# A two-layer diffusion backbone on one core: second-layer attention with pairs of float32r parts, a first modulation in chunks, and a second layer planned late

## The chip, the cores and the metric

The kernel runs on one core of a Trainium2 chip. What counts is the device time of one execution in microseconds: 1668.15 us for the kernel before, the median of 3 runs (1667.54 to 1668.26). In what follows PE is TensorE's matmul stream, PEld its weight loads, DVE VectorE, ACT ScalarE, POOL GpSimd, and SP the engine that issues the DMAs.

## What is computed

Two layers (DEPTH = 2) work on 512 latent tokens and 256 context tokens of width 1024. Cut to what matters here:

```python
for li in range(DEPTH):
    m_lat = jnp.split(s_lat @ w_ada[li] + b_ada[li], 6, axis=-1)      # modulation, from silu(c)
    m_ctx = jnp.split(s_ctx @ w_ada[li] + b_ada[li], 6, axis=-1)
    h  = rms_norm(x, g_mix[li]) * (1.0 + m_lat[1]) + m_lat[0]
    hc = rms_norm(ctx, g_mix[li]) * (1.0 + m_ctx[1]) + m_ctx[0]
    p, pc = h @ w_in[li], hc @ w_in[li]                               # 1024 -> 9 x 256
    y = jnp.concatenate([fourier_mix(p[..., :G]),
                         diff_attention_latent(...),                  # 4 heads, softmax twice, minus lam
                         na_attention_latent(...),                    # 4 heads, neighbourhood + context
                         chunk_gmlp(...)], axis=-1)
    x = x + m_lat[2] * (y @ w_out[li])
    ...                                                               # the context too, in layer 0 only
    h = rms_norm(x, g_ffn[li]) * (1.0 + m_lat[4]) + m_lat[3]
    x = x + m_lat[5] * conv_ffn(h, ...)                               # 1024 -> 2 x 2816 -> 1024
```

Every attention head ends in a product of softmax weights W (queries by keys) with values V (keys by 64).

## The kernel before

**Numbers in two parts.** TensorE takes weights and activations as float32r. To keep float32 accuracy, each operand is split into a rounded part (`hi`, a copy to float32r on ScalarE) and the rest (`lo`, one subtraction on VectorE or GpSimd), and `mm3` makes three matmuls of each product: hi hi, hi lo, lo hi. Weights come as 128x512 tiles through SP's queue into `raw` (4 places), are split by `w_split` into `wq` (6 places) and are used in the order of one list, `wlist`. Each tile costs one ScalarE copy and one subtraction `wq<-raw,wq`, on GpSimd or VectorE. Only the product of softmax weights and values stands apart: `turn` transposes a 128x768 tile of W in blocks of 128x128 and copies it to float32, and `pv` multiplies it by V with plain float32 matmuls, 64 columns each. The profile counts each of those as two matmuls.

**Who sets the order.** Nothing is ordered at run time. While the program is built, a planner (`Sched`) plays all threads (generators such as `Attention.item`, `qk_post`, `unit`) against a table of costs, and writes out the instruction of the thread that could start first, priorities `PR` deciding between those within `slack`. An `Alt` lets it choose the engine: `copy` between ScalarE and VectorE, `sub` between VectorE and GpSimd, `bias_w` being the handicap of VectorE for the weights' subtractions. Each engine then runs its own fixed queue, in order, and waits by semaphores. So an instruction that is late holds up all that stands behind it on its engine.

**The main thread.** The strings `o0` and `o1` name the projections of a layer in PE's order. DK, DQ, DV are keys, queries and values of the differential attention, NK, NQ, NV those of the neighbourhood attention, GU and GV the gated MLP, FA and FC the two halves of Fourier mixing, OO the output projection. A letter behind gives the streams: `l` latent, `c` context, `i` latent then context, `j` context then latent. `unit` runs one of them: for each of 4 latent and 2 context tiles of 128 tokens, 8 chunks of the depth of 128, and 3 matmuls of 256 columns for each chunk. `DKj4` does so in four rounds of two chunks, so that it can begin when two chunks of `h` are there. Attention items run as threads of their own between the matmuls of the main thread. An item is 128 queries of a head: scores, maximum, exponential, transposition, product with V.

**Modulation.** Section s of the modulation is a 1024 x 1024 product with one vector for each stream. At the start `ada_first` brings section 1 (the scale) as rows for TensorE (`ada_rows`: 16 float32 matmuls `plain,svec` of 512 columns with 2 rows out) and section 0 (the shift) as transposed tiles for VectorE (`ada_wide`: a custom multiply-and-sum, `CUSTOM_DVE_ANT_0`, 32 of them), half of the 1024 outputs after the other. All later sections go the VectorE way, one 256 KB tile at each `pace` (every 5.5 us in layer 0, from 64.2 us on, and every 4.1 us for layer 1), two such instructions for a tile when both streams need it.

**Feed-forward.** `up` makes pairs of 128 channels, 3 x 8 matmuls of 512 and as many of 258 columns for each; `conv` and `gated` follow on ScalarE, VectorE and GpSimd. `down` sums groups of four such channels into x. The last `down` of layer 0 and the norm of layer 1 (`Norm`: squares, their sum by matmuls with ones, GpSimd's power, a broadcast by matmuls, then eight chunks) stand between the layers.

## Time and profile before

| what | value |
|---|---|
| median of 3 runs | 1668.15 us |
| the profiled execution: its time | 1666.4 us |
| its span, first to last instruction | 1664.6 us |
| PE busy | 1599.3 us (96%) |
| PEld busy | 1419.3 us (85%) |
| DVE busy | 1103.6 us (66%) |
| ACT busy | 749.1 us (45%) |
| POOL busy | 715.3 us (43%) |
| mean granted clock of TensorE | 0.983 |

The span is 1.8 us short of the execution's own time, and that execution is 1.75 us below the median of the runs. All instructions bear the line of one helper (L314, L329 in the changed kernel), so groups are told apart by operation and tile: `wq,rounded` or `rounded,wq` is a product of weights and activations, `rounded` alone scores, `plain` alone the product of softmax weights and values, `ident` and `identr` transpositions. A row with a busy time gives the sum over the group, then the mean duration of one, which overlaps that of its neighbours.

### The profile page before, as it was taken

The numbers are of one execution on the slowest core, as the hardware profiler recorded it, in microseconds if no ns is written. First come the engines' busy times: TensorE is split into PE (matmuls) and PEld (weight loads), VectorE is DVE, ScalarE is ACT, GpSimd is POOL, SyncE is SP. The second block draws the span as 40 slices with busy tenths as digits, with TensorE's granted clock in tenths as the row PEclk, the third lists the DMA queues.
The fourth block names the chain that finished last, engine by engine and source line by source line (L and its number), as shares of the span: only waits on it lengthen the run. The fifth ranks groups of instructions, "written<-read, shape, count | busy, mean of one in ns | idle before, by whom it ended". The sixth has DMA issues, their size and how long they took to land.

```text
span 1664.6 us, 27016 instructions
## 1 busy us (share of the span) xinstructions
PE 1599.3 (96%) x9932; PEld 1419.3 (85%) x9932; DVE 1103.6 (66%) x2170; ACT 749.1 (45%) x1478; POOL 715.3 (43%) x550
## 2 busy tenths in 40 slices
PE   6799999999898999999999999999999999999999
PEld 2699889998687888888888888899999888888887
DVE  7998997888899856555543359578666744334334
ACT  4447765763523223223132236475665644334331
POOL 4762635345344433323333247214246654444442
PEclk8899999999999999999999998999999999999999
DMA  8331322545344343343421131101325433223222
GB/s 275 122 108 46 102 77 84 169 149 176 109 147 151 124 135 121 128 132 127 122 82 64 63 116 41 51 27 52 115 83 167 158 103 99 95 95 101 95 96 88
DMA packets 101652, 183.03 MB, mean 110 GB/s; under 512 B 12176, under 2 KB 14864, under 8 KB 101520
## 3 DMA queue, kind: packets, MB, share of 16 engines
q1 hardware_dynamic: 101520, 181.31, 33.3%
q8 instruction: 78, 1.28, 0.3%
q14 instruction: 54, 0.44, 0.1%
HBM read 177.07 MB, written 4.19 MB: 109 GB/s over the span
## 4 chain that ended last, share of the span: by engine, by line
PE 75%; DVE 16%; DMA 3%; ACT 2%; issue 2%; POOL 1%; SPq 0%; ACTq 0%; POOLq 0%; DVEq 0%
PE banks L314 75%; DVE plain L314 10%; DVE wa L314 3%; DVE rounded L314 2%; ACT plain L314 1%; POOL wq L314 1%; DMA raw<-in_w_out_dram 1%; DMA wa<-in_w_adat_dram 1%; DVE wq L314 1%; SPq L314 0%; DMA plain<-in_w_adat_dram 0%; ACT wq L314 0%; DMA raw<-in_ffn_up_dram 0%; ACT rounded L314 0%; POOL plain L314 0%
## 5 line engine op out<-in xcount | busy, mean ns | idle before, releaser
L314 PE MATMUL banks<-rounded,wq 128*128 128x512 f32 (+2 forms) x5856 | 1099.4, 348 | 14.5 <-DVE plain L314 9.4
L314 PEld LDWEIGHTS banks<-rounded,wq 128*128 128x128 f32 x5856 | 938.0, 189 | 158.6 <-issue 13.3
L314 POOL TENSOR_TENSOR wq<-raw,wq 128x512 fp32r<-128x512 f32 x390 | 528.2, 1358 | 709.5 <-ACT wq L314 675.3
L314 ACT ACTIVATE wq<-raw 128x512 fp32r<-128x512 f32 x425 | 264.0, 626 | 359.0 <-PE banks L314 260.4
L314 PE MATMUL banks<-wq,rounded 128*128 128x256 f32 (+1 forms) x1980 | 276.1, 295 | 11.0 <-DVE rounded L314 6.0
L314 DVE SCALAR_TENSOR_TENSOR plain<-banks,conv,plain 128x769 f32<-128x769 f32 (+1 forms) x176 | 155.4, 883 | 187.9 <-ACT plain L314 185.4
L314 PEld LDWEIGHTS banks<-wq,rounded 128*128 128x128 f32 x1980 | 254.1, 197 | 18.8 <-DVE rounded L314 6.8
L314 DVE SCALAR_TENSOR_TENSOR plain<-banks,m,plain 128x512 f32<-128x512 f32 (+1 forms) x176 | 112.4, 639 | 160.0 <-PE banks L314 159.7
L314 DVE CUSTOM_DVE_ANT_0 wa<-wa,plain 128x512 f32<-128x512 f32 x160 | 140.3, 878 | 45.3 <-DMA wa<-in_w_adat_dram 43.6
L314 POOL TENSOR_TENSOR plain<-plain,mhalf 128x4 f32<-128x4 f32 (+2 forms) x74 | 95.7, 1298 | 119.2 <-DVE plain L314 92.0
L314 ACT ACTIVATE plain<-banks,conv 128x770 f32<-128x770 f32 (+1 forms) x88 | 77.9, 885 | 138.7 <-PE banks L314 132.5
L314 ACT ACTIVATE plain<-plain 128x256 f32<-128x256 f32 (+3 forms) x152 | 78.7, 536 | 131.9 <-DVE plain L314 122.4
L314 ACT ACTIVATE plain<-banks,plain 128x768 f32<-128x768 f32 (+4 forms) x189 | 112.9, 606 | 54.9 <-PE banks L314 39.7
L314 ACT ACTIVATE plain<-banks 128x256 f32<-128x256 f32 (+2 forms) x217 | 93.3, 445 | 83.7 <-PE banks L314 72.9
L314 DVE TENSOR_TENSOR plain<-plain 128x256 f32<-128x256 f32 (+4 forms) x166 | 110.8, 670 | 19.7 <-ACT plain L314 13.0
L314 ACT ACTIVATE rounded<-plain 128x512 fp32r<-128x512 f32 (+2 forms) x110 | 65.7, 603 | 82.5 <-DVE plain L314 58.1
L314 DVE TENSOR_TENSOR rounded<-plain,rounded 128x256 fp32r<-128x256 f32 (+2 forms) x108 | 88.2, 823 | 17.3 <-ACT rounded L314 16.4
L314 DVE TENSOR_REDUCE plain<-banks 128x1 f32<-128x768 f32 (+4 forms) x112 | 92.0, 835 | 10.6 <-PE banks L314 9.7
L314 DVE CUSTOM_DVE_ANT_0 plain<-wa,plain 128x512 f32<-128x512 f32 x96 | 86.5, 902 | 15.8 <-DMA wa<-in_w_adat_dram 15.7
L314 PE MATMUL banks<-plain 128*128 128x64 f32 x736 | 90.5, 270 | 0.1
L314 PEld LDWEIGHTS banks<-plain 128*128 128x128 f32 x736 | 88.9, 192 | 1.8 <-issue 0.5
L314 POOL TENSOR_TENSOR plain<-plain 128x256 f32<-128x256 f32 (+2 forms) x52 | 61.7, 1196 | 61.8 <-DVE plain L314 27.8
(69 smaller groups left out, 960.9 us busy)
## 6 DMA issues: line engine op xcount, KB each, us to landing
raw<-in_ffn_up_dram SPq DMA_DIRECT2D x184, 256.0 KB, 2.6
wa<-in_w_adat_dram SPq DMA_DIRECT2D x160, 256.0 KB, 2.8
raw<-in_ffn_down_dram SPq DMA_DIRECT2D x88, 256.0 KB, 2.5
raw<-in_w_in_dram SPq DMA_DIRECT2D x80, 256.0 KB, 2.6
raw<-in_w_out_dram SPq DMA_DIRECT2D x64, 256.0 KB, 2.8
plain<-in_na_bias_dram SPq DMA_DIRECT2D x16, 320.0 KB, 3.6
plain<-in_xT_dram SPq DMA_DIRECT2D x16, 256.0 KB, 4.4
plain<-in_w_ada_dram SPq DMA_DIRECT2D x16, 256.0 KB, 4.0
```

Of the source, the lines that this page charges most:

```text
L314: fn(*args, **kw)
```

## The change

**Second-layer attention.** With `pvr[1] = 1`, layer 1 (not layer 0) splits both factors of the product with V. `turn` writes the transposed weights as float32r (`PT`) and adds a subtraction on VectorE for the rest (`PL`), both in one of two fixed places (`pts`). `values` splits V of each head once, hi and lo side by side. `pv` makes two float32r matmuls of each key block, PT by 128 columns (hi and lo of V) and PL by 64, and a `scalar_tensor_tensor` on VectorE adds the two halves. 168 pairs of float32 matmuls become 336 float32r matmuls.

**Side by side.** A new token DP runs keys and values of the differential attention as one projection (`pair_unit`): matmuls of 512 columns for 256 keys and 256 values, in four rounds, in both layers.

**First modulation in chunks.** `start_loader` brings the first two sections in quarters of the outputs, each followed by the weights of one round of DP. The first two quarters go whole to TensorE (512 columns, both sections), the last two by halves (256 columns of section 1 to TensorE, section 0 to VectorE). The latents' x is loaded ahead of the context.

**Second layer planned late.** `later` swaps priorities and rules for all that comes after the last three `up` of layer 0, among them `bias_w` (1.9 before that point, 0.1 behind it; it was 1.0). 35 weight subtractions stood on VectorE and 390 on GpSimd; now 232 and 197 do, 123 of VectorE's in the last feed-forward. The last `down` of layer 0 is listed twice, once for each stream (4 more weight tiles). The pace of the modulation is 5.9 us from 17.8 us on in layer 0, and 4.9 us for layer 1. The planner's cost table has new numbers, and it plans around the case that VectorE and GpSimd both read the memory at once (`port`).

```diff
+     'o0': 'DPi DQi NKl NVl NVc GUj NKc FAj GVj NQj XX FCc FCl OOc OOl', 'lead': 5, 'ffn_s': [1, 0],
+               'ada': 5.31}, 'o1': 'DPj NVj DQl NKi2 GVl NQl GUl2 FAl XX FCl OOa OOb',
...
+    def start_loader(nq):
...
+        for q in range(4):
+            w = 512 if q < NOW["rows"] else 256
+            tiles = []
+            spawn(ada_rows(q, w, tiles), 0.3)
...
+            if w < 512:
+                tiles = []
+                spawn(ada_wide(0, 0, q // 2, 2, tiles, 2, q % 2 * 4, 4), 0.3)
...
+            for i in range(q * nq, (q + 1) * nq):
+                yield from w_load(i, True)
...
+        for ph in range(4):
+            for i, (s, h, t) in enumerate(jobs):
...
+                for k in (2 * ph, 2 * ph + 1):
+                    q = yield from W.get(k)
+                    hk = yield from h.get(k, part)
+                    pairs.append(((hk[0][:, c], hk[1][:, c]), q))
...
+                yield mm3(p, pairs, ph == 0, ph == 3)
...
+                if parts_:
+                    yield sub(PL[:, cs], p[:, 0:n], PT[:, cs], False)
...
+                    two_ = [T.matmul(p[:, 0:128], PT[:, c], self.vp[hd][:, k * 128:k * 128 + 128], start=(j == 0),
+                                     stop=(j == n - 1)),
+                            T.matmul(p[:, 0:64], PL[:, c], self.vp[hd][:, k * 128:k * 128 + 64], start=False, stop=False)]
...
+            if PL is not None:
+                yield V.scalar_tensor_tensor(dst, p[:, 64:128], r, dst, ALU.mult, ALU.add)
```

**Where instructions move, first place.** PE's queue at the start, before: `plain,svec` are the rows of section 1, `ident` the broadcast of the norm (128x128) and the turning of the section's result (128x2), `wq,rounded` the keys, then the values.

```order
L314 MATMUL banks<-plain,svec 2x512 x3
L314 MATMUL banks<-wq,rounded 128x256 x6
L314 MATMUL banks<-plain,svec 2x512 x2
L314 MATMUL banks<-ident,plain 128x128 x4
L314 MATMUL banks<-plain,svec 2x512
L314 MATMUL banks<-wq,rounded 128x256 x6
L314 MATMUL banks<-plain,svec 2x512
L314 MATMUL banks<-ident,plain 128x2 x4
L314 MATMUL banks<-wq,rounded 128x256 x438
```

The same place after the change; `plain,svec` of 2x512 are the first two quarters, of 2x256 the last two, and 128x512 is the new projection DP, of which 102 more matmuls follow the last row.

```order
L329 MATMUL banks<-ones,plain 128x1 x6
L329 MATMUL banks<-plain,svec 2x512 x10
L329 MATMUL banks<-ident,plain 128x2 x4
L329 MATMUL banks<-plain,svec 2x512 x6
L329 MATMUL banks<-ident,plain 128x128 x6
L329 MATMUL banks<-ident,plain 128x2 x4
L329 MATMUL banks<-plain,svec 2x256 x8
L329 MATMUL banks<-ident,plain 128x2 x2
L329 MATMUL banks<-wq,rounded 128x512 x36
L329 MATMUL banks<-plain,svec 2x256 x8
L329 MATMUL banks<-wq,rounded 128x512 x6
L329 MATMUL banks<-ident,plain 128x2 x2
```

A whole round of DP (36 matmuls of 512 columns) now stands ahead of the last quarter of the modulation; before, only 12 matmuls of 256 columns stood ahead of the last row of section 1, and 438 behind it.

**Second place.** PE's queue in the neighbourhood attention of layer 1, before: `rounded` of 256 and 384 columns are scores, `plain` of 64 columns the products with V, and `rounded,wq` of 512 columns matmuls of the Fourier projection FA, put between the items.

```order
L314 MATMUL banks<-rounded,wq 128x512 x6
L314 MATMUL banks<-ident,plain 128x128 x4
L314 MATMUL banks<-rounded 128x384 x2
L314 MATMUL banks<-rounded 128x256 x2
L314 MATMUL banks<-ident,plain 128x128 x4
L314 MATMUL banks<-plain 128x64 x4
L314 MATMUL banks<-identr,rounded 128x128 x8
L314 MATMUL banks<-ident,plain 128x128
L314 MATMUL banks<-identr,rounded 128x128 x6
L314 MATMUL banks<-rounded,wq 128x512 x6
L314 MATMUL banks<-plain 128x64 x5
L314 MATMUL banks<-rounded 128x256 x4
```

After, the same attention from its first scores on:

```order
L329 MATMUL banks<-wq,rounded 128x512 x24
L329 MATMUL banks<-rounded 128x256 x4
L329 MATMUL banks<-rounded 128x384 x2
L329 MATMUL banks<-rounded 128x256 x2
L329 MATMUL banks<-rounded,wq 128x256 x3
L329 MATMUL banks<-identr,rounded 128x128 x8
L329 MATMUL banks<-rounded,wq 128x256 x9
L329 MATMUL banks<-identr,rounded 128x128 x6
L329 MATMUL banks<-rounded 128x384 x2
L329 MATMUL banks<-rounded 128x256 x2
L329 MATMUL banks<-ident,plain 128x128 x4
L329 MATMUL banks<-rounded 128x256 x4
```

The last half of Fourier mixing (the first row) now stands ahead of all 16 items, and from here to their end PE's queue holds 15 matmuls with weights (12 of them in these rows) beside the items' own; the output projection, the next of the main thread, needs the items' results.

**Third place.** VectorE's queue in that same stretch, after the change; `rounded<-banks,rounded` are the new subtractions, `SCALAR_TENSOR_TENSOR` the new sum of the two halves, the first row adds the position bias to the scores, and `TENSOR_REDUCE` is the maximum of a row of scores.

```order
L329 TENSOR_TENSOR banks<-banks,plain 128x384
L329 RECIPROCAL plain<-plain 128x1
L329 TENSOR_TENSOR rounded<-banks,rounded 128x128
L329 SCALAR_TENSOR_TENSOR plain<-banks,plain 128x64
L329 TENSOR_REDUCE plain<-banks 128x1
L329 TENSOR_TENSOR rounded<-banks,rounded 128x512
L329 SCALAR_TENSOR_TENSOR plain<-banks,plain 128x64
L329 CAST rounded<-banks 128x512
```

Before, VectorE had of these only the bias, the maximum, the reciprocal and a part of the copies; the subtractions and sums stand in one queue with them now, so that each waits for its turn there.

## Rows read from the trace of the kernel before

**Rows 1.** The page's busy times of three engines: us, share of span, instructions.

```profile
PE   1599.3 (96%) x9932; PEld 1419.3 (85%) x9932; DVE 1103.6 (66%) x2170; ACT 749.1 (45%) x1478; POOL 715.3 (43%) x550
```

**Rows 2.** Stretches: length, PE, PEld, DVE, ACT, POOL busy us (count), clock, DMA share, GB/s.

```profile
20.00:40.00 20.00, 14.54 (x42) 3.67 (x43) 18.57 (x42) 6.57 (x14) 13.66 (x13) 0.83 0.90 296
40.00:60.00 20.00, 11.34 (x41) 5.70 (x41) 19.57 (x34) 6.54 (x11) 18.55 (x13) 0.74 0.57 186
...
100.00:380.00 280.00, 273.71 (x2207) 261.69 (x2206) 245.49 (x625) 187.16 (x469) 128.45 (x107) 1.00 0.34 109
...
440.00:560.00 120.00, 111.42 (x626) 95.82 (x627) 117.06 (x206) 39.00 (x54) 54.42 (x32) 1.00 0.44 139
...
980.00:1060.00 80.00, 70.45 (x480) 66.50 (x479) 62.41 (x143) 41.02 (x82) 46.25 (x33) 0.89 0.23 79
1060.00:1320.00 260.00, 254.26 (x2035) 245.28 (x2034) 186.32 (x381) 168.37 (x374) 107.00 (x87) 0.99 0.28 93
1320.00:1664.60 344.60, 340.02 (x1509) 281.45 (x1507) 145.46 (x179) 131.47 (x211) 158.24 (x122) 1.00 0.29 99
```

**Rows 3.** PE in order of time, the start: start, length, matmuls, [idle before <-releaser].

```profile
27.65 1.02 PE L314 MATMUL banks<-plain,svec 128*2 128x512 f32 x2
...
35.57 1.87 PE L314 MATMUL banks<-plain,svec 128*2 128x512 f32 x2 [0.71 <-DMA plain<-in_w_ada_dram]
...
58.73 16.51 PE L314 MATMUL banks<-wq,rounded 128*128 128x256 f32 x119 [0.74 <-DVE rounded L314]
```

**Rows 4.** PE in order of time: two unbroken streams, and the neighbourhood attention's ends.

```profile
74.83 38.08 PE L314 MATMUL banks<-wq,rounded 128*128 128x256 f32 x316
...
376.68 41.16 PE L314 MATMUL banks<-rounded,wq 128*128 128x512 f32 x186
...
1182.16 0.84 PE L314 MATMUL banks<-rounded 128*128 128x384 f32 x4
...
1235.51 1.00 PE L314 MATMUL banks<-plain 128*128 128x64 f32 x8
```

**Rows 5.** DVE in order of time: two equal instructions of the first modulation.

```profile
16.80 0.69 DVE L314 CUSTOM_DVE_ANT_0 plain<-plain 128x512 f32<-128x512 f32 x1
...
48.45 1.76 DVE L314 CUSTOM_DVE_ANT_0 plain<-plain 128x512 f32<-128x512 f32 x1
```

**Rows 6.** What PE waited for, 440 to 560 us: sum, times, longest.

```profile
PE banks L314 <- DVE plain L314: 8.1, 5, 1.7
```

**Rows 7.** The page's costliest groups: the later modulation on VectorE.

```profile
L314 DVE CUSTOM_DVE_ANT_0 wa<-wa,plain 128x512 f32<-128x512 f32 x160 | 140.3, 878 | 45.3 <-DMA wa<-in_w_adat_dram 43.6
```

**Rows 8.** What PE waited for, 980 to 1060 us.

```profile
PE banks L314 <- DVE plain L314: 4.1, 2, 3.4
PE banks L314 <- DVE wq L314: 3.0, 2, 2.3
```

**Rows 9.** PE groups by form, 990 to 1320 us: count, busy, mean ns, idle before.

```profile
L314 PE MATMUL banks<-plain 128*128 128x64 f32 x336 | 40.7, 270 | 0.0
L314 PE MATMUL banks<-ident,plain 128*128 128x128 f32 x220 | 36.0, 283 | 1.2 <-POOL plain L314 1.1
...
L314 PE MATMUL banks<-rounded 128*128 128x256 f32 x48 | 8.7, 291 | 0.0
...
L314 PE MATMUL banks<-identr,rounded 128*128 128x128 f32 x56 | 5.6, 248 | 0.0
L314 PE MATMUL banks<-rounded 128*128 128x384 f32 x16 | 4.5, 363 | 0.0
```

**Rows 10.** DVE groups by form, 990 to 1320 us.

```profile
L314 DVE TENSOR_TENSOR plain<-plain 128x256 f32<-128x256 f32 x44 | 26.8, 614 | 9.3 <-ACT plain L314 6.0 <-POOL plain L314 3.0
L314 DVE TENSOR_TENSOR wq<-raw,wq 128x512 fp32r<-128x512 f32 x21 | 20.6, 979 | 16.7 <-ACT wq L314 16.5
...
L314 DVE TENSOR_TENSOR rounded<-banks,rounded 128x512 fp32r<-128x512 f32 x8 | 5.4, 687 | 4.7 <-ACT rounded L314 4.7
...
L314 DVE TENSOR_SCALAR plain<-banks,plain 128x64 f32<-128x64 f32 x5 | 1.4, 284 | 4.0 <-PE banks L314 4.0
```

More of the change, by code (lines that the diff above doesn't have):

```diff
@@ L619, in ada_fin, with ada_wide @@
             done.add((li, sec, c))
[L621 removed]
+    def ada_wide(li, sec, hf, ns, tiles, step=4, i0=0, n=8):
         acc_ = yield sm()
@@ L627, in ada_wide @@
             prod = yield k2()
-        for i in range(8):
-            yield lambda: len(tiles) > i and sbc[0] is not None
-            t = tiles[i]
+        for i in range(i0, i0 + n):
+            yield lambda: len(tiles) > i - i0 and sbc[0] is not None
+            t = tiles[i - i0]
             for st in range(ns):
@@ L737, in one @@
                 yield lambda: self.x[k] is not None
-                for j in range(self.parts):
-                    yield from self.add(k, j)
+                yield from self.add(k, 0, False)
             for k in range(8):
-                spawn(one(k), 0.5)
+                spawn(one(k), 0.1)
         def finish(self):
@@ L1177, in gate, with pt_slots @@
         left[0] -= 1
-    heads, items = Tokens(P["heads"]), Tokens(P["items"])
+    pts, at_work = [], {}
+    def pt_slots(li):
+        if NOW["pvr"][li]:
+            at_work[li] = 4 if li == 0 else 2
+            for i in range(NOW["slots"]):
+                pts.append((yield Req(sr, 1536, F32R)))
+    heads, items = Tokens(NOW["heads"]), Tokens(NOW["items"])
     class Attention:
@@ L1704, in start1, with later @@
         attn_all(1)
-    act(start1)
-    for tok in P["o1"].split():
-        token(1, tok)
-    ffn(1)
-    act(lambda: n1[1][0].drop_h())
+    def later():
+        NOW.update(P["later"])
+        PR.update(NOW["pr"])
+        n0[1] = [Norm(1, 0, s, drop=True, parts=1 if s else NOW["parts"][1]) for s in (0, 1)]
+        n1[1] = [Norm(1, 1, 0, parts=NOW["parts"][2])]
+        ffn(0, NOW["tail"] or [("down", 4), ("down", 5)])
+        act(start1)
+        tokens(1)
+        ffn(1)
+        act(lambda: n1[1][0].drop_h())
+        closed.append(True)
+    act(ada1)
+    ffn(0)
     def main():
```

372 lines of the change are left out of this document (247 added, 125 removed).

## The prediction

> **What bounds the kernel now.** The page's busy times come first: PE is at work for 1599 of 1665 us, and no other engine for more than 1104 [rows 1]. So the time is PE's work, plus the time in which PE stands still, plus what a lower clock costs, and each has to be found in its place. The table by stretches [rows 2] shows three such places. From 20 to 60 us PE is busy for 26 of 40 us, at a granted clock of 0.74 to 0.83, while the DMAs move 296 and then 186 GB/s: the start. From 440 to 560 us PE misses 8.6 us, and VectorE is busy for 117 of 120: the head of the first feed-forward, beside the modulation for layer 1. From 980 to 1060 us PE misses 9.6 us at a clock of 0.89: the change of layers. In the rest, 100 to 380 and 1060 to 1320 us, where all the attention is, PE misses 2% only, because weight products stand between the attention items; the last stretch is PE alone. A gain must come from the three places or from cheaper matmuls; a loss can come wherever PE stops being covered. The sum below is made against the profiled execution, 1666.4 us (span 1664.6 and 1.8 around it); the median of the runs is 1.75 above it.
>
> **1. The start, in chunks: -12 us.** Before, PE's unbroken stream starts at 58.7 us with 17 of the 288 matmuls of keys and values done [rows 3]. The next 119 last to 75.2, and the other 152 go at 38.08 / 316 = 120.5 ns [rows 4]: 18.3 us more, so keys and values are through at 93.2. After, the queue reads: 16 float32 rows of 512 columns, the norm's broadcast, 8 rows of 256 columns, a round of DP. VectorE is done with the sums of squares at 16.8 in both orders, since that takes all of x and ctx (its next instruction starts there [rows 5]). From 17 on the 16 rows take 1.02 us each when they follow each other, as the row at 27.65 does [rows 3]: 34. Broadcast and turning: 37. The 8 half rows: 41. The first chunks of h have by then gone through GpSimd, ScalarE and VectorE, which I put at 45. Then 144 matmuls at 41.16 / 186 = 221 ns [rows 4] are 31.9 us, and the last 8 half rows within them 4.1: 81. That is 12 us sooner, and the cheaper form of the projection is in it (288 x 120.5 against 144 x 221 ns: 2.9 us). The data allow it: by 45 us the queue must have brought x, ctx, three quarters of the modulation and two rounds of weights, some 11 MB; 296 GB/s [rows 2] bring 12 in 42 us. Ends: if the rows run at the 1.87 us of the row at 35.57 [rows 3], 13.6 us more, a loss of 2; if h is ready at 41, a gain of 16.
>
> **2. VectorE behind the start: +3 us.** Between 100 and 380 us VectorE is busy for 245 of 280 us [rows 2]. The change leaves its work in layer 0 about as it was (16 instructions of the first modulation less, 11 of the later sections more, a dozen others). The same 245 us in 12 us less are 92%. PE misses 2% at VectorE's 88% there and 7% at its 98% from 440 to 560 us [rows 2]; 92% lies at some 3%, and 1% more of 280 us is 3. Ends are 0 and all 12.
>
> **3. Head of the feed-forward: -6 us.** There PE waits 8.1 us for VectorE [rows 6]. Layer 1's modulation takes two instructions of 0.88 us [rows 7] for each tile there; a tile each 4.9 instead of 4.1 us takes 0.36 instead of 0.43 of VectorE, 8 us in the 120. The wait should nearly go. Next late is PE itself, so no more than 8.6 can be had; 0 is the other end.
>
> **4. Change of layers: -6 us.** 9.6 us idle and a clock of 0.89 on 70 busy us are some 17 us of loss [rows 2]. PE waits there for VectorE's norm (4.1 us) and for weight tiles that VectorE splits (3.0) [rows 8]. The norm's chain stays. But DP needs two chunks of h and two weight tiles for each round of 36 x 221 ns = 8 us, where the keys alone needed four chunks in each half. And the last `down`, listed twice, no longer holds four of the six places of split weights. Its four more tiles are hidden, at a DMA share of 0.23. I take a third of the loss; ends 0 and -12.
>
> **5. DP in layer 1: -3 us.** 288 x 120.5 - 144 x 221 ns = 2.9 us of PE, as in step 1.
>
> **6. The product with V: -6 us.** 336 float32 matmuls take 40.7 us [rows 9], 242 ns for a pair. No row has a float32r matmul of 128 or 64 columns on freshly loaded values. Nearest is the transposition `identr`, 128 float32r columns against a fresh 128x128 operand: 5.6 / 56 = 100 ns. Two of them make 200 ns, and 168 x 42 ns = 7 us; as 64 columns can hardly be dearer and accumulation may be, I take 6. Ends: each as dear as a 256-column matmul, 120.5 ns, gives 0; 192 columns at the 221 / 512 ns of the long stream give 83 ns for the two and a gain of 27. The Trainium skill ("TensorE: Matmul & The Clock Gate", section "Back-to-back issue gap") gives 81 ns as the sustained spacing of matmuls of 128 columns; by that this step would be worth 13 us, an estimate that the 100 ns of the row speak against.
>
> **7. Layer 1's attention: +13 us.** Here the change turns against itself. *VectorE's load.* From 1060 to 1320 us it is busy for 186 of 260 us [rows 2]. Added: some 50 of the 64 weight subtractions that come from GpSimd before layer 1's feed-forward, at up to 0.98 us, 50; 56 new subtractions from PSUM, at 0.69 us for 512 columns and less for the shorter ones, 31; 32 sums of halves, for which a 64-column operation at 0.28 is the nearest row, 9. Taken away: 21 additions of 256 columns at 0.61, which go to GpSimd, 13 [rows 10]. That makes 263 of 260. The price of 0.98 has GpSimd's weights beside it, though; at the 0.69 us of a subtraction of 512 columns from PSUM [rows 10], 84 weight subtractions are 24 us cheaper: 239. Such a load, 92 to 101%, is what the trace has from 440 to 560 us, where PE misses 7%. Over the first attention half, 130 us, that is 9 us against some 3 now. *The cover.* The neighbourhood items, from 1182 to 1236 us [rows 4], have weight products between them now; after, 15 such matmuls are left for 16 items. PE's own work on the items is 13.2 us of scores, 42 transpositions at 0.10, 80 at 36.0 / 220 = 0.164, 144 products at 0.10 [rows 9] and 1.8 for the 15: 47 us. The items took 54 us with VectorE less loaded, and nothing is queued behind but the output projection, which needs all of them. I put the stretch at 54 to 57, so PE stands still for 7 to 10 us where it did not before. Together 13 to 16, of which I take the lower; ends 0 and 30.
>
> **8. At no price.** In layer 1's feed-forward 121 weight subtractions move to VectorE: 118 us at 0.98 onto 145 busy of 345 [rows 2], a load of 76% beside a PE that is never short of weights there. If that cover failed, each late tile would cost what the split took, under 1 us.
>
> Sum: -12 + 3 - 6 - 6 - 3 - 6 + 13 = -17. 1666.4 - 17 = 1649.4, and 1.75 for the median: 1651. Its own range, from the middle halves of the ends, is 1643 to 1660.
>
> **Rivals.** *The attention stays covered.* VectorE's multiply-and-sum takes 0.69 us alone and 1.76 us at 48 us, when GpSimd is busy for 18.6 of 20 [rows 2, 5]. With most weights off GpSimd, VectorE's other work in layer 1 may shrink as much as the new work adds, and step 7 is 0: 1638. The Trainium skill ("SBUF — State Buffer", section "Who interferes with whom") says that a VectorE instruction with two inputs in SBUF waits for a GpSimd one that reads SBUF, for its whole length; by that rule just this happens, and the two rows agree with it. Against it stand the missing matmuls between the items, which no faster VectorE brings back. 17 in 100.
>
> *VectorE is layer 0's clock.* It is at 88% from 100 to 380 us and at 98% behind it. If it, not PE, sets when layer 0's attention and the first channels end, steps 1 to 3 bring nothing: 1668 - 6 - 3 - 6 + 13 = 1666. For it speaks that its work hardly shrinks; against it that PE misses only 6 us of 280 there. 12 in 100.
>
> *The chunks bring no earlier stream*, since rows at the slow price and DMA waits fill the time to 58 us: without step 1, and nothing to give back, 1660 to 1663. 8 in 100.
>
> *Slower: the clock falls in the uncovered items.* At the start, with PE waiting for DMAs and chunks, the granted clock was 0.74 [rows 2], near to halfway between TensorE's levels of 1.2 and 2.4 GHz. If the 16 items of layer 1 run at the lower level, their 47 us of PE work become 94, some 37 above the 57: 1688. It turns into a loss as soon as half of the stretch runs so. 8 in 100.
>
> **How the numbers follow.** The forecast, 1651, has 55 in 100. About 0.2%, 3.3 us, can be told from no change, so faster is below 1664.8. Forecast, covered attention and late chunks lie below (80), with a third of VectorE's clock (4): 84. Of the rest, 8 are the same (6 of VectorE's clock, 2 of the falling clock) and 8 slower. From 1634 (the covered attention with cheaper products) to 1667 some 84 in 100 are held.
>
> **What would show it.** Right: an unbroken PE stream of 512 columns from 40 to 50 us on, DP done by 77 to 86; under 4 us of waits for VectorE in the head of the feed-forward; 34 us for the 336 new matmuls; VectorE above 90% from layer 1's first scores on, and PE below 90% busy in the 16 items. Wrong: PE busy throughout the items (first rival), waits for VectorE above 5% in layer 0's attention (second), rows of 1.87 us at the start (third), a granted clock below 0.9 in the items (fourth).

## The result and the profile after

The changed kernel takes 1679.44 us (median of 4 runs, 1676.59 to 1684.48), beside 1667.85 us for the kernel before on the same chip: a ratio of 1.0081, 95% interval 1.0064 to 1.0098. It is slower, by 11.6 us; 1651 was forecast, and the range ended at 1667. The profiled execution took 1680.2 us with a span of 1678.2, which is 13.6 longer than the span before.

The busy times of the page, which answer to [rows 1]: us, share of the span, instructions.

```profile
PE 1618.5 (96%) x9680; PEld 1422.7 (85%) x9680; DVE 1191.3 (71%) x2438; ACT 748.2 (45%) x1478; POOL 480.8 (29%) x386
```

PE has 252 matmuls fewer and is busy for 19 us longer. The same stretches of the kernel after as in [rows 2], with the same columns:

```profile
20.00:40.00 20.00, 20.00 (x59) 5.45 (x59) 4.17 (x11) 4.75 (x9) 1.31 (x2) 0.86 0.74 243
40.00:60.00 20.00, 13.27 (x53) 9.07 (x52) 19.86 (x31) 8.30 (x17) 19.84 (x16) 0.91 0.51 164
100.00:380.00 280.00, 272.99 (x2194) 261.30 (x2193) 249.49 (x669) 187.99 (x464) 135.51 (x112) 1.00 0.36 115
440.00:560.00 120.00, 119.81 (x682) 105.76 (x683) 104.47 (x191) 42.58 (x57) 46.61 (x32) 1.00 0.42 132
980.00:1060.00 80.00, 75.92 (x403) 65.95 (x402) 59.83 (x137) 39.30 (x76) 32.76 (x25) 0.94 0.26 85
1060.00:1320.00 260.00, 242.68 (x1819) 228.99 (x1818) 214.15 (x486) 163.74 (x372) 64.38 (x70) 0.93 0.25 83
```

The head of the feed-forward is full now (440 to 560 us), the change of layers nearly so, and from 1060 to 1320 us PE misses 17.3 us at a clock of 0.93, where it missed 5.7 at 0.99 before. Six marks, found by counting PE's matmuls in both traces, tell where the 13.3 us up to the last matmul come from:

| mark | before, us | after, us | ahead (-) or behind |
|---|---|---|---|
| keys and values of layer 0 done | 93.5 | 90.1 | -3.4 |
| first `up` of layer 0 | 416.2 | 412.7 | -3.5 |
| feed-forward of layer 0 done | 994.3 | 985.9 | -8.4 |
| layer 1 has 288 x 256 columns of projections behind it | 1050.1 | 1030.0 | -20.1 |
| last matmul of the 576 with 256 columns in layer 1 (output projection, first `up`) | 1322.5 | 1336.9 | +14.4 |
| last matmul | 1660.9 | 1674.2 | +13.3 |

So all that was gained, 20 us, and 14 more, is lost between the fourth and the fifth mark, and there in layer 1's attention. The stretch from the fourth mark to the last product with V, before and after:

```profile
1050.10:1236.50 186.40, 186.35 (x1525) 180.14 (x1524) 133.34 (x302) 124.11 (x288) 53.98 (x46) 1.00 0.17 55
```

```profile
1030.00:1259.00 229.00, 214.83 (x1566) 200.38 (x1565) 190.30 (x466) 139.84 (x324) 60.26 (x61) 0.93 0.18 62
```

Read such a row as a sum: 229.0 - 214.8 = 14.2 us in which PE stood still, 214.8 x (1 - 0.93) = 15.0 us that the lower clock cost, and 199.8 us that the same matmuls take at the full clock. (The two stretches hold somewhat different work, and a clock of two decimals leaves about 1 us open.) Over the whole of layer 1 up to the fifth mark, PE's standing still goes from 15.3 to 22.9 us, the clock's cost from 8.5 to 21.3, the rest from 304.4 to 306.8. Where the clock fell, the rows just before and behind the fall and PE's own order of time read:

```profile
1165.00:1169.00 4.00, 2.47 (x16) 2.02 (x16) 3.93 (x10) 2.52 (x8) 1.01 (x1) 1.00 0.00 0
1169.20:1193.10 23.90, 20.84 (x90) 19.39 (x91) 16.77 (x52) 8.73 (x20) 9.15 (x10) 0.50 0.03 12
```

```profile
1165.26 0.85 PE L329 MATMUL banks<-rounded 96*128 96x512 f32 x3 [0.29 <-ACT plain L329]
1167.38 1.68 PE L329 MATMUL banks<-rounded 96*128 96x256 f32 x13 [1.26 <-DVE rounded L329]
1169.59 1.09 PE L329 MATMUL banks<-ident,plain 128*128 128x128 f32 x4 [0.53 <-DVE plain L329]
1171.08 0.69 PE L329 MATMUL banks<-ident,plain 128*128 128x128 f32 x2 [0.40 <-DVE plain L329]
1174.04 1.12 PE L329 MATMUL banks<-ident,plain 128*128 128x128 f32 x4 [2.28 <-DVE plain L329]
1174.81 2.80 PE L329 MATMUL banks<-rounded 128*128 128x128 f32 x12
...
1180.27 2.80 PE L329 MATMUL banks<-rounded 128*128 128x128 f32 x12
...
1184.88 2.80 PE L329 MATMUL banks<-rounded 128*128 128x128 f32 x12
```

PE waits twice, for 0.3 and 1.3 us, and from 1169.2 us on the granted clock is at 0.50, the lower level of 1.2 GHz, for 23.9 us. The next three waits, of 0.5, 0.4 and 2.3 us for VectorE, stand behind the fall already. A product with V takes 2.80 us there; at 1094 us it took 1.46. These are the last of the differential items, where the weight products between them have run out. What PE waited for in the whole stretch (sum, times, longest):

```profile
PE banks L329 <- DVE rounded L329: 5.2, 9, 1.6
PE banks L329 <- DVE plain L329: 4.8, 6, 2.3
PE banks L329 <- ACT plain L329: 3.2, 6, 0.9
```

### The profile page after: what moved, and what is told of

The parts are those of the page before. It is cut to its first block, busy times and chain, and to the rows that moved or that the text cites. A ratio compares the mean times of both kernels' runs of the same rounds, so it can differ in the third digit from the quotient of the medians.

```text
span 1678.2 us, 26520 instructions
## 1 busy us (share of the span) xinstructions
PE 1618.5 (96%) x9680; PEld 1422.7 (85%) x9680; DVE 1191.3 (71%) x2438; ACT 748.2 (45%) x1478; POOL 480.8 (29%) x386
## 4 chain that ended last, share of the span: by engine, by line
PE 66%; DVE 5%; ACT 1%; issue 1%; POOL 1%; DVEq 0%; ACTq 0%; POOLq 0%
PE banks L329 66%; DVE plain L329 3%; DVE rounded L329 1%; ACT plain L329 1%; DVE wq L329 1%; POOL plain L329 0%; ACT L329 0%; ACT rounded L329 0%; POOL rounded L329 0%; ACT wq L329 0%; DVE banks L329 0%; DVEq L329 0%; ACTq L329 0%; POOLq L329 0%
## 5 line engine op out<-in xcount | busy, mean ns | idle before, releaser
L329 POOL TENSOR_TENSOR wq<-raw,wq 128x512 fp32r<-128x512 f32 x197 | 276.2, 1408 | 414.2 <-ACT wq L329 386.2
L329 PE MATMUL banks<-wq,rounded 128*128 128x256 f32 (+1 forms) x1692 | 262.0, 309 | 3.3 <-DVE m L329 1.2
L329 PEld LDWEIGHTS banks<-wq,rounded 128*128 128x128 f32 x1692 | 233.4, 192 | 19.8 <-ACT plain L329 1.3
L329 DVE TENSOR_TENSOR wq<-raw,wq 128x512 fp32r<-128x512 f32 x232 | 165.9, 718 | 55.3 <-ACT wq L329 54.7
L329 POOL TENSOR_TENSOR plain<-plain 128x256 f32<-128x256 f32 (+1 forms) x61 | 57.7, 951 | 440.3 <-DVE plain L329 321.2
L329 PE MATMUL banks<-rounded 128*128 128x128 f32 (+5 forms) x624 | 108.3, 311 | 7.8 <-DVE rounded L329 5.3
L329 PEld LDWEIGHTS banks<-rounded 128*128 128x128 f32 (+1 forms) x624 | 87.4, 201 | 12.7 <-DVE rounded L329 5.8
L329 PE MATMUL banks<-ident,plain 128*128 128x128 f32 (+1 forms) x500 | 84.5, 291 | 13.4 <-DVE plain L329 9.5
L329 ACT ACTIVATE plain<-banks 128x256 f32<-128x256 f32 (+3 forms) x164 | 67.4, 425 | 66.8 <-PE banks L329 60.1
L329 POOL TENSOR_TENSOR rounded<-plain,rounded 128x256 fp32r<-128x256 f32 (+3 forms) x48 | 54.0, 1130 | 142.7 <-ACT rounded L329 68.4
```

Source lines behind the costliest of these rows:

```text
L329: fn(*args, **kw)
```

## The experiments

Fifteen kernels were run, each the kernel after with the edit shown (x12 and x13 stand on x8). The planner sets the order anew for each of them, so that two runs differ by their order beside the edit. All times stand beside runs of the kernel before on the same chip, whose median was 1666.1 to 1666.6 us (1667.85 for the kernel after). The last four columns are of the attention stretch of layer 1 defined above, worked out of one row each as for the kernel after.

| run | product in layer 1, order | us | ratio to before [95%] | length | PE still | clock | rest |
|---|---|---|---|---|---|---|---|
| kernel after | pairs | 1679.4 | 1.0081 [1.0064, 1.0098] | 229.0 | 14.2 | 15.0 | 199.8 |
| x1 | float32 | 1663.6 | 0.9978 [0.9965, 0.9991] | 212.4 | 6.0 | 8.3 | 198.1 |
| x8 | float32, items first | 1653.0 | 0.9916 [0.9889, 0.9943] | 202.7 | 3.6 | 2.0 | 197.1 |
| x13 | float32, items first, GV late | 1653.5 | 0.9912 [0.9894, 0.9929] | 203.4 | 4.7 | 2.0 | 196.7 |
| x3 | float32, plan of before | 1661.6 | 0.9966 [0.9953, 0.9980] | 203.5 | 5.2 | 2.0 | 196.3 |
| x7 | as x3, no pair DP | 1666.9 | 1.0005 [0.9992, 1.0018] | 206.8 | 7.3 | 2.0 | 197.5 |
| x11 | float32 and 56 subtractions | 1674.6 | 1.0053 [1.0033, 1.0072] | 226.8 | 15.2 | 12.7 | 198.9 |
| x10 | pairs, high part only | 1661.3 | 0.9967 [0.9953, 0.9980] | 212.1 | 16.3 | 11.7 | 184.1 |
| x4 | pairs, weights to GpSimd | 1682.8 | 1.0099 [1.0072, 1.0126] | 223.7 | 14.5 | 8.4 | 200.8 |
| x9 | pairs, items first | 1683.4 | 1.0099 [1.0081, 1.0117] | 231.0 | 12.5 | 19.7 | 198.8 |
| x6 | pairs, low part copied | 1693.6 | 1.0167 [1.0150, 1.0184] | 237.9 | 17.5 | 19.8 | 200.6 |
| x14 | pairs, items first, GU and GV late | 1697.7 | 1.0183 [1.0161, 1.0205] | 238.6 | 15.2 | 29.0 | 194.4 |
| x5 | pairs, three places | 1711.1 | 1.0276 [1.0255, 1.0298] | 257.8 | 21.5 | 37.8 | 198.5 |
| x2 | pairs, plan of before | 1726.4 | 1.0364 [1.0349, 1.0380] | 270.0 | 25.4 | 44.0 | 200.6 |

The last column hardly moves (x10 leaves matmuls out, x14 has other sections in the stretch). Of the 67 us in length between x8 and x2, 64 are PE standing still and the clock that falls with it. And the new product costs 16 us with the priorities of the kernel after (against x1), 30 with the items first (x9 against x8), 65 with the plan of before (x2 against x3): its price depends on the order around it.

**The product alone (x1).**

```diff
+P['pvr'] = [0, 0]
```

> The kernel after with one edit: layer 1's product with V is the float32 one of the kernel before (no subtractions of the low part from PSUM, no sums of halves, no two places for the parts); weights, priorities and the rest as after. Theory PRODUCT (layer 1's attention lost its 38 us because the new product loads VectorE and has only two places): the stretch from the end of keys and values of layer 1 to the end of the first half of its output projection shrinks from 254 us to about 230, and the time to some 1658 to 1664. Theory PLAN (what is missing is cover: the order that the new priorities give leaves the neighbourhood items without weight products, whichever product they use): the items keep their waits, 4 to 5 us come off with the VectorE work and as much is added on TensorE, and the time stays within 1674 to 1684.

It gave 1663.6: theory PRODUCT, and faster than the kernel before. The row:

```profile
1028.80:1241.20 212.40, 206.38 (x1565) 195.07 (x1564) 160.38 (x383) 133.71 (x301) 52.26 (x48) 0.96 0.21 67
```

**The plan of the kernel before (x2, x3), and its two sections in place of the pair (x7).**

```diff
+P['later'].update(slack=0.1, bias_w={'DVE': 1.0}, tail=[],
+    o1='DPj DQl NVj GVl NQl NKi GUl2 FAl XX FCl OOa OOb',
+    pr={'d': 5.88, 'n': 0.01, 'g': 7.6, 'gate': 6.26, 'w': 5.94, 'y': 6.97, 'conv': 2.77, 'gated': 8.24, 'main': 8.4,
+        'f': 2.81, 'fm': 3.04, 'ad': 0.48, 'an': 0.01, 'ada': 8.75})
```

This is x2. x3 has `P['pvr'] = [0, 0]` besides, and x7 has x3's lines with `o1='DKj2 DQl DVj NVi GVl NQl NKi GUl2 FAl XX FCl OOa OOb'`.

> The kernel after with layer 1 planned by the priorities, the slack, the list of sections (DP in place of DK and DV) and the weight bias of the kernel before (weights split on GpSimd); the new product stays. Theory PLAN: cover comes back with the old order, so the neighbourhood items run beside weight products, layer 1's attention takes 216 to 225 us instead of 254, time 1643 to 1655. Theory PRODUCT: the order changes little, since the new product with its two places and its VectorE work holds the attention items up: layer 1's attention stays at 245 to 260 us, time 1670 to 1685.

> The kernel after with layer 1 planned by the priorities, slack, list and weight bias of the kernel before, and with the float32 product: what is left of the change is layer 0 (start in chunks, its sections, modulation) and DP in layer 1. Both theories expect layer 1's attention at 212 to 220 us, as before, and keep the 8 us gained up to the end of layer 0's feed-forward: 1650 to 1658 if the shorter change of layers stays too, 1658 to 1664 if that belonged to the new plan. If the losses of layer 1 came from the layers' new starting state (buffers, DP's chunks) and neither from product nor priorities, it is 1672 or more.

> As the run with the early plan and the float32 product (1661.6 us), but keys and values of the differential heads of layer 1 are two sections as in the kernel before, and no pair. If the pair is worth what steps 4 and 5 said at the change of layers (2.9 us of TensorE and fewer waits there), it is 7 to 11 us slower than that run: 1668 to 1673. If what the pair brings at the change of layers is given back in the attention behind it (TensorE waits there for values and weights that come no sooner), within 3 us of 1661.6.

Neither theory had x2 at 1726 us. Weight products are counted here, and below, in PE's order from the first transposition of layer 1's queries and keys to the last product with V, at 221 ns for 512 columns. In x2 64 us of them stand ahead of the end of the first tenth of the products with V, and 12 among the other nine tenths (x3: 13 and 64). The items are then alone, PE stands still for 25 us and runs at a mean clock of 0.82:

```profile
1032.50:1302.50 270.00, 244.59 (x1565) 223.07 (x1564) 190.87 (x458) 140.66 (x322) 79.52 (x70) 0.82 0.17 52
```

x3 came out at 1661.6, in its second expectation but not for the reason given there: the change of layers stays short (47.3 us, 55.8 before), and part of the gain is lost again behind it, with 5.2 us of standing still and 2.0 of clock where the kernel before has none. x7 lies 5.3 us above x3, between the two expectations. From the end of layer 0's feed-forward to the fourth mark it takes 51.2 us, x3 47.3: the pair is worth 3.9 us there, 2.9 of which is the cheaper matmul by step 5's estimate.

**VectorE's load (x4).**

```diff
+P['later']['bias_w'] = {'DVE': 0.6}
```

> The kernel after with one number of layer 1's plan changed, the weight bias 0.1 to 0.6: 34 more of layer 1's 210 weight subtractions go to GpSimd, the order of TensorE stays about as it was and the items have no more cover. If VectorE's load (84 of 95 us busy from 1065 to 1160) is what holds layer 1's attention, 25 us less of it are worth 6 to 12 us: 1667 to 1674. If the missing cover alone does it, within 4 us of 1679.

1682.8 us, no gain. As a test of VectorE's load it is weak, though: most of the subtractions that moved lie outside the stretch, where VectorE is busy for 187.4 us in place of 190.3.

**Places (x5), and the low part on ScalarE (x6).**

```diff
+P['later']['slots'] = 3
+P['slots'] = 3
```

```diff
-                    yield sub(PL[:, cs], p[:, 0:n], PT[:, cs], False)
+                    yield copy(PL[:, cs], p[:, 0:n])
```

> The kernel after with three places instead of two for the parts of turned probabilities; nothing else is edited, the order is planned anew. Theory PLACES (an item holds its place from its turning to its product, so with two places only two items can be between the two, and TensorE waits): of the 9.8 us that TensorE stands still between 1065 and 1205 us, and the 4.4 in the neighbourhood items, more than half goes, and with it the half clock there: 1666 to 1672. Theory CHAIN (each item has become longer by a subtraction from PSUM and a sum, and the cover is what it was): within 4 us of 1679.

> The kernel after, where the low part of the turned probabilities is a second copy from PSUM (by ScalarE for the most part) instead of VectorE's subtraction of the high part: this part of the computation is changed, the low part is not the difference. TensorE's instructions stay as they are, VectorE loses most of 56 subtractions (37 us of work), and the low part no longer waits for the high one. Theory CHAIN (the subtractions on VectorE, in line behind the other items' maxima and sums, are what TensorE waits for): 1665 to 1671. Theory PLACES: the places are given back a little earlier, 1673 to 1678. If the whole loss comes from the two other new things, the product itself and the sums of halves: within 3 us of 1679.

Both fell outside all expectations, on the slow side. A third place lets the planner put items closer together and further from the weight products: again stretches of items alone, at a mean clock of 0.84. So a third place did not help with the order that the planner made for it; the run can't price a place by itself. In x6 VectorE is busy for 179.5 us in the stretch, 11 less, and PE stands still no less; the wait changes its name, from VectorE to ScalarE:

```profile
PE banks L329 <- ACT plain L329: 7.9, 11, 1.8
PE banks L329 <- ACT rounded L329: 3.5, 7, 0.8
PE banks L329 <- DVE plain L329: 1.8, 6, 0.4
```

**The subtraction added to the float32 product (x11), and taken from the pairs (x10).**

First x11, then x10:

```diff
+P['pvr'] = [0, 0]
...
-                if parts_:
-                    yield sub(PL[:, cs], p[:, 0:n], PT[:, cs], False)
+                if parts_ or self.li:
+                    yield sub(PL[:, cs] if parts_ else p[:, 0:n], p[:, 0:n], PT[:, cs], False)
```

```diff
-                if parts_:
-                    yield sub(PL[:, cs], p[:, 0:n], PT[:, cs], False)
...
-                            T.matmul(p[:, 0:64], PL[:, c], self.vp[hd][:, k * 128:k * 128 + 64], start=False, stop=False)]
+                            ][0:1]
```

> The first run (float32 product, 1663.6 us) with the 56 subtractions of the new product put back, written over the PSUM bank that they read and used by nobody: work is added, nothing else is changed. Theory SECOND EVICTION: the items become as late as in the kernel after, with its waits and its half clock: 1674 to 1682. If it is the product's places, values or sums: 1662 to 1668.

> The kernel after, where the turned probabilities have a high part only: this part of the computation is left out, the 56 subtractions from PSUM and the 168 matmuls of 64 columns that use the low part. The places, the copies of the values in parts and the sums of halves stay. TensorE has 168 x 0.107 = 18 us less to do, so the bare sum is 1661. Theory SECOND EVICTION (each turning leaves PSUM by two instructions, on whichever engine, and that is what makes the items late): the waits and the half clock go too, 1645 to 1655. If they come from the sums or the places: 1657 to 1664.

x11 is the clearest of the runs. The same product as in x1, with a subtraction that nobody reads behind each turning, brings back 10.9 of the 15.8 us between x1 and the kernel after, and all of the standing still:

```profile
1027.20:1254.00 226.80, 211.63 (x1566) 199.32 (x1565) 180.30 (x423) 136.66 (x311) 56.82 (x54) 0.94 0.19 62
```

```profile
PE banks L330 <- DVE banks L330: 7.0, 8, 1.6
```

```profile
1166.22 1.55 PE L330 MATMUL banks<-plain 128*128 128x64 f32 x12 [1.56 <-DVE banks L330]
1184.93 2.82 PE L330 MATMUL banks<-plain 128*128 128x64 f32 x12 [1.19 <-DVE banks L330]
```

`DVE banks` is that subtraction: while it runs its bank is not free, and PE's next use of a bank waits, a product with V (as in the last two rows) in six of the eight cases and 5.3 of the 7.0 us, a transposition in two. But the planner's order is another one too: at the end of the fourth tenth of the products with V, 47 of the 59 us of weight products are used up in x11, 35 in x1 and 44 in the kernel after. How much of the 10.9 us is the subtraction and how much that order, no run separates.

x10 came out as the other theory said, 1661.3: with the subtraction go 18 us of matmuls by the estimate (15.7 by the last column), and 16.3 us of standing still and 11.7 of clock stay. A shorter item on PE is also a shorter cover for the next item's work on VectorE and ScalarE; that this is why x10 gained nothing more was argued, not shown, and the sums and places that x10 keeps may have their part in it.

**Cover: items first (x8, x9), and sections held back (x13, x14).**

```diff
+P['pvr'] = [0, 0]
+P['later']['pr'].update(an=0.01, ad=0.48, main=8.4)
+P['later'].update(slack=0.1)
```

This is x8; x9 is without the first line. x13 adds `o1 = 'DPj NVj DQl NKi2 NQl GVl GUl2 FAl XX FCl OOa OOb'` to x8. x14 has the second line alone, and `o1 = 'DPj NVj DQl NKi2 NQl FAl GVl GUl2 XX FCl OOa OOb'`.

> The kernel after with the float32 product in layer 1 (as the first run, 1663.6 us) and three priorities and the slack of layer 1 as in the kernel before: attention items ahead of the sections, so that weight products remain for the neighbourhood items (12 us of them in place of 0.3 behind the middle of layer 1's products with V). Theory COVER (what the first run still loses against before, some 6 us from the first section of layer 1 to its eighth `up` half, are its uncovered items: 3.9 us of standing still in 44, and a clock of 0.72 from 1160 to 1190): 1654 to 1659. If cover is worth nothing, 1661 to 1666.

> The kernel after, new product kept, with the three priorities and the slack of the run with float32 items first (1653.0 us): the fourth of two products by two sets of priorities. If the product and the priorities act apart, the priorities bring the same 10.6 us as with the float32 product: 1667 to 1671. If the new product takes the cover away whatever the priorities (in its order no weight product stands behind the second third of layer 1's products with V, where the float32 order has 10 us of them), the neighbourhood items wait and their clock falls as in the kernel after: 1675 to 1695.

> The run with float32 items first (1653.0 us) with one section moved in layer 1's list: GV behind NQ, so that 19 us of weight products stand behind the second half of the items in place of 10, and 11 of them in the last tenth. If cover is still what is missing there, 1646 to 1651; it had 0.2 us of standing still in that stretch, so if cover is enough already, 1651 to 1656.

> The kernel after, new product kept, with the three priorities of the items-first runs and a list of layer 1's sections that keeps GV and GU until the last: 33 us of weight products lie between the neighbourhood items and the end of the differential ones, and 8 within the differential ones, where the kernel after has 29. If the loss is the new product's slower items wherever they are uncovered, it moves from the one to the other: the neighbourhood items run without waits, the differential ones at half clock, 1675 to 1700. If only the neighbourhood items needed cover, as step 7 had it, 1664 to 1670.

With the float32 product the priorities bring 10.6 us more, and x8 beats both kernels: 1653.0 us. PE hardly waits any more, and the clock stays up:

```profile
1033.10:1235.80 202.70, 199.07 (x1566) 188.48 (x1565) 161.44 (x380) 131.43 (x298) 60.44 (x54) 0.99 0.21 70
```

```profile
PE banks L332 <- ACT plain L332: 1.9, 6, 0.5
```

x13, with more of the cover behind the second half of the items, is no faster: there was enough. With the pairs the same priorities bring nothing (x9). The planned order has only 1.6 us of weight products behind the first six tenths of the products with V, as was expected, but the neighbourhood items are not where most is lost: in the differential items PE stands still for 7.5 us and loses 17 by the clock (x8: 3.4 and 2), in the neighbourhood items 5.1 and 2. At the end of the third tenth 43 of the 59 us of weight products are used up (x8: 21). x14 forces cover into the neighbourhood items: PE stands still there for 3 us in place of 6, but in the differential items, now bare, for 12 in place of 8, and the clock costs 22 us there in place of 9. Cover in the one place is no cure, since the cover is the same 59 us wherever it lies.

**The start (x12, x15).** x12 is x8 with `P['rows'] = 4`; x15 is the kernel after with

```diff
-                yield V.tensor_tensor_reduce(t if st == ns - 1 else prod, t,
-                                             sbc[0][:, st * D + (i % 2) * 512:st * D + (i % 2) * 512 + 512], 1.0, 0.0,
+                m = 128 if n < 8 else 512
+                yield V.tensor_tensor_reduce((t if st == ns - 1 else prod)[:, 0:m], t[:, 0:m],
+                                             sbc[0][:, st * D + (i % 2) * 512:st * D + (i % 2) * 512 + m], 1.0, 0.0,
```

> The run with float32 items first (1653.0 us) with all four quarters of layer 0's first modulation as rows of 512 columns on TensorE, none by halves on VectorE; read at the end of layer 0's keys and values, which is at 86 to 90 us in the kernel after and all runs so far, against 81 in step 1. If the last two quarters are late because VectorE has their other half and is behind, keys and values end at 81 to 85 us. If they are late because the modulation's tiles and the weights come in no sooner, at 88 to 93.

> The kernel after, where VectorE's 16 multiply-and-sums of the first modulation's last two quarters take 128 of their 512 columns: this part of the computation is cut to a quarter, some 14 us of VectorE between 42 and 75 us. Read at the end of layer 0's keys and values (90.1 us in the kernel after, 86 to 88 in its offspring, 81 in step 1). If VectorE, busy for 19.9 of 20 us from 40 to 60 us, is what the chunks wait for: 79 to 83. If it is GpSimd (19.8 of 20) or the transfers: 85 to 89. The time follows by the same amount, 1670 to 1675 or 1676 to 1680.

Keys and values of layer 0 end at 92.4 us in x12 (1655.1 us in all) and at 89.3 in x15: with VectorE's sums cut, and GpSimd busy for 14.7 us in place of 19.8 from 40 to 60, nothing is gained. That leaves the transfers, and what they wait for. Its time, 1695.2, says nothing more, since layer 0's order behind the start came out different: the first `up` is 12 us late. What stands in the way is in the trace of the kernel after. PE's order of time, and that of SP's queue:

```profile
46.36 9.96 PE L329 MATMUL banks<-wq,rounded 128*128 128x512 f32 x36 [1.17 <-DVE m L329]
59.62 5.30 PE L329 MATMUL banks<-plain,svec 128*2 128x256 f32 x16 [3.30 <-DVE plain L329]
64.85 1.66 PE L329 MATMUL banks<-wq,rounded 128*128 128x512 f32 x6
```

```profile
31.71 2.52 SPq L329 DMA_DIRECT2D plain<-in_w_ada_dram  x2
...
48.88 0.91 SPq L329 DMA_DIRECT2D wa<-in_w_adat_dram  x2
55.87 3.34 SPq L329 DMA_DIRECT2D plain<-in_w_ada_dram  x2
```

```profile
SPq L329 <- DVE rounded L329: 8.9, 2, 6.0
```

The rows of the last quarter are issued at 55.9 us, 24 after those of the third; SP's queue has just stood still for 6.0 us for a place in `plain`, and PE, whose order has those 16 rows ahead of the next weight products, starts them at 59.6. The DMAs move 164 GB/s from 40 to 60 us, after 243. That the place is the cause is read from the trace; no run has a place more there.

## Why the prediction was wrong

The sum said -17 us against the profiled execution; the spans say +13.6. Steps 6 and 7 (+7 put, +34.5 measured) make some 27 of the 31 us between the two.

**Step 1, the start: -12 put, -3.4 measured.** The order of events was right (the first round of DP at 46.4 us, put at 45), as was that of the half rows. The failed sentence is that the data allow it: it counted bytes by the rate of [rows 2], and left out that the queue is in order and waits for places. The last quarter came 24 us after the third. PE's wait for it is 3.3 of the 9 us between 81 and 90.1, though. The 144 matmuls took 35 us where 31.9 were put, most of that in the first 36, and the half rows 5.2 where 4.1 were put; both ran in part at the lower clock, which the step left out (the clock is the third number from the end):

```profile
46.36:56.32 9.96, 9.96 (x36) 7.78 (x36) 9.86 (x15) 1.42 (x4) 9.96 (x8) 0.84 0.30 91
59.62:64.85 5.23, 5.23 (x17) 1.56 (x17) 5.23 (x8) 3.84 (x8) 2.84 (x3) 0.67 0.60 208
```

In the thirteen other runs whose start has the same order (all but x12 and x15), keys and values end at 86.0 to 89.2 us. So the profile of the kernel after shows the latest of them, and the start gains 3 to 8 us, not 12.

**Step 2, +3 put, 0 measured.** The 3.4 us are still there at the first `up`, though VectorE is busy for 249 of 280 us. So the second rival, VectorE as layer 0's clock, is out as well.

**Step 3, -6 put, -4.9 measured (8.4 less 3.5).** PE's wait for VectorE in the head of the feed-forward is gone, as was said. **Steps 4 and 5, -9 put, -11.7 measured**; x7 and x3 give the pair 3.9 of it. **Step 8 was right**: the feed-forward of layer 1 takes 337.3 us, 338.5 before, with 121 more subtractions on VectorE.

**Step 6, the product: -6 put, 0 at best.** The kernel before has a row that would have settled it, and I read a group's busy time in its place ([rows 9], 242 ns for a float32 matmul). First a group of six float32 matmuls before (two records each, and what follows it), then six pairs after:

```profile
1082.67 1.45 PE L314 MATMUL banks<-plain 128*128 128x64 f32 x12
1083.96 0.39 PE L314 MATMUL banks<-ident,plain 128*128 128x128 f32 x2
```

```profile
1094.09 1.46 PE L329 MATMUL banks<-rounded 128*128 128x128 f32 x12
1095.38 0.84 PE L329 MATMUL banks<-ident,plain 128*128 128x128 f32 x6
```

Both keep PE for 1.29 us: 215 ns for a float32 matmul of 64 columns, 107 ns for each matmul of the pair. The 242 ns hold overlap with the neighbours; the 100 ns from `identr` were nearly right, and the error was in the other number. "Ends: 0 and a gain of 27" had the answer as its end. The Trainium skill ("TensorE: Matmul & The Clock Gate", section "Back-to-back issue gap") gives 81 ns for 128 columns; the trace has 107, and the measurement decides. What both groups have in common is the number of weight loads, before and after:

```profile
1082.56 1.43 PEld L314 LDWEIGHTS banks<-plain 128*128 128x128 f32 x12
1093.98 1.43 PEld L329 LDWEIGHTS banks<-rounded 128*128 128x128 f32 x12
```

Twelve loads take 1.43 us in either. The columns differ (12 x 64 before, 6 x 128 and 6 x 64 after), the loads and the time do not, so in these two groups the price goes with the loads and not with the columns; no run changes the loads alone.

**Step 7, layer 1's attention: +13 put, some +34 measured with step 6** (the fourth mark at -20.1, the fifth at +14.4). Its own quantity came near: PE stands still for 14.2 us where it did not before. But that is luck in part, since the places are others: 7 to 10 us were put into the 16 neighbourhood items. There, first in the kernel after, then in x1 with the float32 product, whose items have the same 15 matmuls with weights between them:

```profile
1211.30:1259.00 47.70, 43.29 (x344) 40.73 (x343) 42.80 (x106) 32.35 (x83) 2.10 (x4) 0.96 0.28 94
1196.00:1241.20 45.20, 41.29 (x344) 38.49 (x344) 29.49 (x69) 30.17 (x73) 0.00 (x0) 1.00 0.29 100
```

PE stands still for 4.4 us in the one and 3.9 in the other, so the missing cover costs the old product nearly as much there. What the new product adds lies ahead of these items, for the most part in the differential ones: 9.8 us of standing still, 2.1 in x1.

Three things were not in the step. The clock: 15.0 us in the stretch. I had it as the last rival with 8 in 100, in the neighbourhood items; most of it fell earlier, in the last differential items, where I had taken cover for granted, and behind waits of 0.3 and 1.3 us, not in one long standstill. The product, which gives nothing back. And the kind of cause: I reckoned VectorE's load (92 to 101%; it is 190 of 229 us, 83%) and took it for the price. (The lower end counts 84 weight subtractions, the upper one 71; with 71 it is 93%. From 1060 to 1320 us the trace has 55.) By load, x6 (179.5 us) should stand still less than the kernel after (190.3), and x2 (190.9) no more; they stand still for 17.5 and 25.4 us, beside 14.2. x11 shows that a second instruction between a turning and its free bank, with the order that the planner makes for it, is enough to bring the waits back; x10 shows that they can stay without it. That the length of the way from one use of a bank to the next decides, once no weight product covers it, fits these runs but is argued, not shown.

**The rivals.** The first (VectorE gets quicker beside an idle GpSimd, and the attention stays covered) was half right. Of the weight subtractions on VectorE the group from 1030 to 1260 us reads 786 ns, for 979 in [rows 10], and GpSimd is busy for 26% of the stretch, against 41% in [rows 2]:

```profile
L329 DVE TENSOR_TENSOR wq<-raw,wq 128x512 fp32r<-128x512 f32 x31 | 24.3, 786 | 8.4 <-ACT wq L329 8.4
```

The Trainium skill ("SBUF — State Buffer", section "Who interferes with whom") says that such an instruction, with two inputs in SBUF, waits for a GpSimd one that reads SBUF, and the two means agree with it. It did not keep the attention covered. The last rival, the falling clock, is what came, at another place and with less than half of its price.

**What stays open.** How much of the new product's price is the subtraction itself and how much the order that the planner makes around it. Whether sums and places of the new product cost something beside its subtraction (x10 leaves room for that, x5 can't tell), and some 2 us by which the pairs come out dearer on PE in the last column (198.5 to 200.8 against 196.3 to 198.9), little more than what the rounding of the clock leaves open. Nor was it tried to give the start one more place.

## What to carry to other kernels

Price a matmul by the distance from a group's first instruction to the next group's in the order of time; a group's busy time counts overlaps and can hide that two forms cost the same. Where items of a chain run without independent matmuls between them, ask how many instructions stand between one use of a bank and the next (the waits of x11 point there, x10 shows that it is not all), and price a standstill above its length, since the clock falls with it (by 0.6 to 1.9 times the standstill in the runs that stood still for over 12 us). A change whose parts each look good is best tried part by part: here the start, the modulation, the pair and the late plan with the old product and items first are worth 0.8%, and the new product alone, with the order planned for it, turned that into a loss (x9).

## What the runs showed of the hardware

In the kernel after, PE stood still for 0.3 and 1.3 us, with 0.85 us of matmuls between and 1.68 behind, and the granted clock went to 1.2 GHz for 23.9 us. At that level a group of six pairs took 2.80 us for 1.46. The runs in which PE stood still for over 12 us in layer 1's attention lost 8 to 44 us by the clock besides, the others 2 to 8 (table above).

A float32 matmul of 64 columns keeps TensorE as long as two float32r matmuls of 128 and 64 columns, each with a weight load of its own: 215 ns (12 loads in 1.43 us in either group of six). So for such small products the split in two parts buys no time on TensorE.
